# The state-space stage of an encoder trunk: the order of three engines written out in the source, in place of the scheduler's

## The chip, the cores and the metric

The kernel runs on one core of a Trainium2 chip. Its time is the device time of one execution in microseconds (us). TensorE multiplies matrices, VectorE, ScalarE and GpSimd work on tiles in the on-chip memory, and SyncE issues the transfers. In the profile they are PE, DVE, ACT, POOL and SP.

## The reference

A trunk of two layers over 512 tokens of width 1024. Layer 0 is attention of two kinds, layer 1 a bidirectional state-space mixer (Mamba-2 SSD); a squared-ReLU MLP follows each, and each residual sum is normalised. The change is in layer 1's mixer:

```
z, xbc, dt = split(x @ w_in)
xs, bm, cm = split(silu(conv5(xbc)))          # 32 heads of 64, 8 groups, state 128
dt = softplus(dt + dt_bias);  a = dt * -exp(a_log)
per direction (forward, backward), chunks of 128 tokens, acum = cumsum(a):
  y_diag = ((C B^T) * exp(acum_l - acum_s), masked) @ (xs * dt)
  states = B^T (xs * dt * exp(acum_end - acum))
  prev   = scan over chunks: prev * exp(acum_end) + states
  y_off  = exp(acum) * (C @ prev)
y = y_f + y_b + xs * d_skip;  y = rmsnorm_per_group(y * silu(z)) * norm_w;  return y @ w_out
```

## The kernel before

Everything lies transposed (features on partitions, the 512 tokens along the free axis). Each float32 operand is split into a high and a low part (`w_hi` on ScalarE, line 69; `w_lo` on VectorE or, for some listed chunks, GpSimd, line 70), and each product is three matmuls (lines 209 to 211). Weight chunks are prepared three ahead, in four buffers.

The input projection is a stream of *steps*: one step is the three matmuls of one contraction block (`project_steps`), eight steps make one 128 x 512 tile. The function `stream` issues the projections of the group after the current one and, behind each, the five-tap convolution (`conv`, line 801 on ScalarE and four instructions of line 803 on VectorE) and the SiLU. The state-space work of the eight groups is put between these steps: `wait()` runs the stream up to the next number in `times` and then issues the next piece of the group's matmuls. A group has 48 steps, the first has more.

A group's pieces in their order are: the product of B and C (line 1031, copied to `cb`); transposes of B (`btok`) and of the two x tiles (`xtok`); `xw`, x weighted by decay and step (line 1054); the states of the three chunk borders (line 1064) with their running sum `pv` (line 1072 on GpSimd, line 1075 on VectorE); four products with the states (line 1006), each multiplied by the decay rows `r` (line 1009); two products within the chunks (line 1016) of `xtok` and `m`, which is `cb` times a decay matrix `e` (line 997); the sum `y` (lines 1019 to 1022); the gate with `z` (line 1106); and the group's normalisation (`scaled`), spread over the next group: squares summed into `q` (line 925), matmuls of the sums, `rstd`, a trip through memory (`rs_d`) to get a row on all partitions, and the scaling of line 961.

A decay matrix `e` is made for each of a group's four heads by `decay_inner`: two loads of `r` from memory (line 872), a mask added on GpSimd (`tb`, line 876), eight exponentials on ScalarE (line 882), and a sum on GpSimd (line 884). `decay_rows` loads and exponentiates the rows `r` (lines 901 and 903).

TensorE's order is the order of the source (`manual_schedule` around the whole body). The order on VectorE, ScalarE, GpSimd and SyncE is chosen by the framework's scheduler when the kernel is built; only ScalarE's table functions are chained in source order by `pin`.

## Time and profile before

| | |
|---|---|
| time, median of 3 runs | 1491.42 us (1489.56 to 1492.58) |
| the profiled execution | 1490.02 us, span 1488.2 us |
| mean granted TensorE clock | 0.977 of full speed |
| TensorE busy | 1407.4 us, 95% |
| VectorE busy | 847.3 us, 57% |
| ScalarE busy | 638.3 us, 43% |
| GpSimd busy | 368.6 us, 25% |

The span runs from the first to the last instruction of the profile. The state-space stage lies between about 620 and 1070 us of it. A granted clock of 1.00 is 2.4 GHz, and a stretch with a mean below 1 ran in part at 1.2 GHz. "Busy" for TensorE takes in matmuls at the low clock, which last longer.

### The profile page before, as it was taken

The numbers are of one execution on the slowest core, as the hardware profiler recorded it, in microseconds if no ns is written. First come the engines' busy times: TensorE is split into PE (matmuls) and PEld (weight loads), VectorE is DVE, ScalarE is ACT, GpSimd is POOL, SyncE is SP. The second block draws the span as 40 slices with busy tenths as digits, with TensorE's granted clock in tenths as the row PEclk, the third lists the DMA queues.
The fourth block names the chain that finished last, engine by engine and source line by source line (L and its number), as shares of the span: only waits on it lengthen the run. The fifth ranks groups of instructions, "written<-read, shape, count | busy, mean of one in ns | idle before, by whom it ended". The sixth has DMA issues, their size and how long they took to land.

```text
span 1488.2 us, 18931 instructions
## 1 busy us (share of the span) xinstructions
PE 1407.4 (95%) x7200; PEld 1160.5 (78%) x7200; DVE 847.3 (57%) x1231; ACT 638.3 (43%) x1117; POOL 368.6 (25%) x255
## 2 busy tenths in 40 slices
PE   8899998999999999987988998999998999999998
PEld 7777778888888888866766876777888888888886
DVE  4677577344343337577678678767467344343336
ACT  5688633323132231467466556645414323142220
POOL 1354221000000121065354466353323100000000
PEclk9999999999999999999999999989999999999999
DMA  8322255223143212374443434432436333133101
GB/s 283 102 95 65 69 198 170 88 97 100 57 127 99 79 43 74 109 184 120 129 127 110 128 113 132 111 97 66 151 97 227 99 99 99 57 127 99 57 1 57
DMA packets 62403, 161.50 MB, mean 109 GB/s; under 512 B 9612, under 2 KB 19624, under 8 KB 62312
## 3 DMA queue, kind: packets, MB, share of 16 engines
q1 hardware_dynamic: 62312, 160.29, 34.4%
q8 instruction: 57, 0.93, 0.2%
q14 instruction: 34, 0.28, 0.1%
HBM read 154.87 MB, written 5.39 MB: 108 GB/s over the span
## 4 chain that ended last, share of the span: by engine, by line
PE 41%; DVE 8%; ACT 4%; issue 2%; DMA 1%; POOL 1%; SPq 0%; DVEq 0%; ACTq 0%; POOLq 0%
PE mm L209 10%; PE mm L210 9%; PE mm L211 9%; PE b L211 2%; PE b L210 2%; PE b L209 2%; DVE xw L1054 2%; PE aux L1064 2%; ACT tb L882 2%; DVE xs L803 1%; PE y L1006 1%; DVE w_lo L70 1%; PE y L1016 1%; DVE m L997 1%; DMA q<-rs_d 1%
## 5 line engine op out<-in xcount | busy, mean ns | idle before, releaser
L69 ACT ACTIVATE w_hi<-w_raw 128x1024 fp32r<-128x1024 f32 (+1 forms) x220 | 231.3, 1053 | 548.4 <-PE mm L210 244.1
L209 PE MATMUL mm<-hi,w_hi 128*128 128x512 f32 (+2 forms) x1112 | 429.8, 387 | 0.6 <-ACT hi L231 0.5
L210 PE MATMUL mm<-lo,w_hi 128*128 128x512 f32 (+2 forms) x1112 | 419.1, 377 | 10.8 <-DVE lo L232 10.8
L211 PE MATMUL mm<-hi,w_lo 128*128 128x512 f32 (+2 forms) x1112 | 417.3, 375 | 0.0
L70 DVE TENSOR_TENSOR w_lo<-w_raw,w_hi 128x1024 fp32r<-128x1024 f32 (+1 forms) x182 | 230.6, 1269 | 294.7 <-ACT w_hi L69 289.9
L210 PEld LDWEIGHTS mm<-lo,w_hi 128*128 128x128 f32 (+1 forms) x1112 | 212.3, 191 | 44.9 <-DVE lo L232 11.5
L209 PEld LDWEIGHTS mm<-hi,w_hi 128*128 128x128 f32 (+1 forms) x1112 | 212.2, 191 | 41.0 <-issue 5.5
L211 PEld LDWEIGHTS mm<-hi,w_lo 128*128 128x128 f32 (+1 forms) x1112 | 211.3, 190 | 39.5
L70 POOL TENSOR_TENSOR w_lo<-w_raw,w_hi 128x1024 fp32r<-128x1024 f32 (+1 forms) x38 | 92.3, 2434 | 445.4 <-ACT w_hi L69 442.2
L209 PE MATMUL mm<-w_hi,hi 128*128 128x512 f32 x352 | 141.1, 401 | 5.9 <-ACT hi L171 5.2
L211 PE MATMUL mm<-w_hi,lo 128*128 128x512 f32 x352 | 139.3, 396 | 0.0
L210 PE MATMUL mm<-w_lo,hi 128*128 128x512 f32 x352 | 139.2, 396 | 0.0
L210 PE MATMUL b<-w_lo,hi 128*128 128x512 f32 (+1 forms) x328 | 123.5, 377 | 1.2 <-DVE w_lo L70 1.2
L209 PE MATMUL b<-w_hi,hi 128*128 128x512 f32 (+1 forms) x328 | 123.6, 377 | 0.4 <-DVE res L310 0.4
L211 PE MATMUL b<-w_hi,lo 128*128 128x512 f32 (+1 forms) x328 | 123.5, 376 | 0.0
L336 POOL TENSOR_TENSOR rstd<-ve,half 128x1 f32<-128x1 f32 x16 | 13.7, 854 | 330.9 <-DVE neg L334 312.2
L876 POOL TENSOR_TENSOR tb<-r,dmask 128x1024 f32<-128x1024 f32 x32 | 84.0, 2626 | 25.7 <-DMA r<-ac_d 24.4
L209 PEld LDWEIGHTS mm<-w_hi,hi 128*128 128x128 f32 x352 | 66.9, 190 | 20.8 <-ACT hi L171 5.2
L211 PEld LDWEIGHTS mm<-w_hi,lo 128*128 128x128 f32 x352 | 66.7, 189 | 15.8 <-DVE lo L232 0.4
L882 ACT ACTIVATE tb<-tb,ac_tok 128x128 f32<-128x128 f32 x256 | 77.6, 390 | 0.6 <-POOL tb L876 0.5
L210 PEld LDWEIGHTS mm<-w_lo,hi 128*128 128x128 f32 x352 | 66.8, 190 | 14.1
L384 DVE TENSOR_TENSOR sq<-relu 128x512 f32<-128x512 f32 x64 | 60.3, 943 | 28.7 <-ACT relu L382 28.7
(279 smaller groups left out, 1860.5 us busy)
## 6 DMA issues: line engine op xcount, KB each, us to landing
w_raw<-in_w_m_dram SPq DMA_DIRECT2D x128, 512.0 KB, 3.6
w_raw<-in_w_ssm_dram SPq DMA_DIRECT2D x48, 512.0 KB, 3.6
r<-ac_d SPq DMA_DIRECT2D x64, 256.0 KB, 4.2
w_raw<-in_w_so_dram SPq DMA_DIRECT2D x16, 512.0 KB, 3.7
w_raw<-in_w_att_dram SPq DMA_DIRECT2D x14, 512.0 KB, 5.4
r<-ac_d SPq DMA_DIRECT2D x64, 96.0 KB, 3.1
w_raw<-in_w_ao_dram SPq DMA_DIRECT2D x8, 512.0 KB, 3.6
xraw<-in_xT_dram SPq DMA_DIRECT2D x8, 256.0 KB, 6.6
```

Source lines behind the costliest of these rows:

```text
L69: split = [nc.scalar.activation(hi[:, cols], raw[:, cols], AF.Copy), eng.tensor_tensor(lo[:, cols], raw[:, cols], hi[:, cols].bitcast(F32) ...
L70: eng.tensor_tensor(lo[:, cols], raw[:, cols], hi[:, cols].bitcast(F32), op=ALU.subtract)]
L209: PE.matmul(ps, lhs_h, rhs_h, start=first, stop=False)
L210: PE.matmul(ps, lhs_h, rhs_l, start=False, stop=False)
L211: PE.matmul(ps, lhs_l, rhs_h, start=False, stop=last)
L384: DVE.tensor_tensor(s, r, r, op=ALU.mult)
L803: DVE.scalar_tensor_tensor(acc[:, lo_o:lo_o + n], ps[:, lo_i:lo_i + n], cw[:, i, k:k + 1], acc[:, lo_o:lo_o + n], op0=ALU.mult, op1=ALU.add)
L876: POOL.tensor_tensor(x, r.rearrange("p d (c l) -> p d c l", c=NT), bc(dmask.unsqueeze(2), [P, 2, NT, P]), op=ALU.add)
L882: pin(ACT.activation(x[:, d, c, :], x[:, d, c, :], AF.Exp, bias=ac_tok[:, c, 32 * d + hf:32 * d + hf + 1]))
L997: DVE.tensor_tensor(m, cb, es[h], op=ALU.mult)
L1054: DVE.tensor_tensor(t, x_tok[j][:, d:d + 3, :].rearrange("p c (h e) -> p c h e", h=2), bc(wdec[:, d:d + 3, hd:hd + 2].unsqueeze(3), [P, 3, ...
L1064: PE.matmul(ps[:, d * 256 + j * P:d * 256 + j * P + P], b_tok[:, c, :], xw[j, d][:, c - d, :, :].rearrange("p h e -> p (h e)"), start=True ...
```

## The change

In the state-space stage VectorE, ScalarE and GpSimd now also run in source order (`manual_schedule` with four engines around `ssd`); SyncE does not. So that source order can differ from the order in which the code reads, pieces of work are queued by `later(step, fn)` and issued when the stream has reached that step (`due`). `decay_inner` and `decay_rows` become lists of pieces with steps for loading, masking, exponentiating and summing. SiLUs, gates, `xw`, `m` and the parts of the normalisation get steps of their own. The steps of TensorE's pieces move: in a group from the second on, the three chunk states go from 13, 13 and 18 to 18, 19 and 22 and the four products with the states from 27, 27, 37 and 38 to 30, 31, 39 and 40. In the output projection that follows, the first split of `y` stays ahead of the sweep and the next eight, which stood there with it, are issued one every third step. The arithmetic stays the same.

```
+        at = [0]
+        tasks = []
+        def due():
+            while tasks and tasks[0][0] <= at[0]:
+                tasks.pop(0)[2]()
+        def later(step, fn):
+            tasks.append((step, len(tasks) and max(t[1] for t in tasks) + 1, fn))
+            tasks.sort(key=lambda t: t[:2])
+        def fill_to(n):
+            while at[0] < n:
+                due()
+                next(steps, None)
+                at[0] += 1
+            due()
...
-                    z = wk.tile([P, T], F32, name="z", bufs=2)
-                    pin(ACT.activation(z, zs[j], AF.Silu))
-                    tiles["z", g, j] = z
+                    later(base + (0 if g == 0 else 33 if g < G - 1 else 2 + 6 * j), lambda g=g, j=j, ps=zs[j]: gate(g, j, ps))
                 if g == 0:
                     for j in range(2):
                         yield from convolved(j, "xs", 4, ("x", 0, j))
-                        silu(tiles["x", 0, j])
+                        later(at[0] + 6, lambda j=j: silu(("x", 0, j)))
                     yield from convolved(17, "bt", 2, ("b", 1))
                     yield from convolved(25, "ct", 2, ("c", 1))
                 if g + 1 < G:
-                    silu(tiles["b", g + 1])
-                    silu(tiles["c", g + 1])
+                    for n in "bc":
+                        later(base + (41 if g == 0 else 34), lambda n=n, g=g: silu((n, g + 1)))
                     for j in range(2):
                         yield from convolved(2 * (g + 1) + j, "xs", 4, ("x", g + 1, j))
-                        silu(tiles["x", g + 1, j])
+                        later(base + (38, 46)[j], lambda j=j, g=g: silu(("x", g + 1, j)))
...
+        def decay_inner(g, h, load, mask, exp, total):
+            hf = 4 * g + h
+            v = {}
+            def loads():
+                v["r"] = wk.tile([P, 2, T], F32, name="r", bufs=2)
                 for d in range(2):
+                    nc.sync.dma_start(out=v["r"][:, d, :],
                                       in_=ac_d[32 * d + hf:32 * d + hf + 1, :].partition_broadcast(P))
+            def masks():
+                v["x"] = wk.tile([P, 2, NT, P], F32, name="tb", bufs=2)
+                POOL.tensor_tensor(v["x"], v["r"].rearrange("p d (c l) -> p d c l", c=NT),
                                    bc(dmask.unsqueeze(2), [P, 2, NT, P]), op=ALU.add)
+            def exps(d, c):
+                pin(ACT.activation(v["x"][:, d, c, :], v["x"][:, d, c, :], AF.Exp,
+                                   bias=ac_tok[:, c, 32 * d + hf:32 * d + hf + 1]))
+            def sums():
+                es[g, h] = wk.tile([P, NT, P], F32, name="e", bufs=6)
+                POOL.tensor_tensor(es[g, h], v["x"][:, 0], v["x"][:, 1], op=ALU.add)
+            later(load, loads)
+            later(mask, masks)
+            for i in range(8):
+                later(exp + i // 2, lambda i=i: exps(i // NT, i % NT))
+            later(total, sums)
...
+        fill_to(12)
+        dt_sums()
+        later(30, dt_exps)
+        for g in range(G):
+            o = 16 + 48 * g
+            if g == 0:
+                for h, at_steps in enumerate(((14, 20, 31, 36), (15, 23, 35, 40), (25, 37, 40, 45), (26, 41, 45, 50))):
+                    decay_inner(0, h, *at_steps)
+                decay_rows(0, 0, 30, 47)
+                decay_rows(0, 1, 31, 48)
+                decay_inner(1, 0, 38, 46, 50, 56)
+                decay_inner(1, 1, 42, 51, 64, 69)
+                decay_rows(1, 0, 55, 69)
+                decay_rows(1, 1, 60, 69)
+                continue
+            if g > 1:
+                decay_rows(g, 1, o - 6, o + (20 if g == G - 1 else 1))
+            n = 4 if g in (1, G - 1) else 0
+            for h in range(2):
+                p = o + 5 * h + n
+                decay_inner(g, 2 + h, o - 7 + 4 * h, p, p + 6, p + 11)
+                if g + 1 < G:
+                    decay_inner(g + 1, h, p + 7, p + 12, p + 17, p + 22)
+            if g + 1 < G:
+                decay_rows(g + 1, 0, o + 20, o + 31)
...
-            times = iter(tuple(352 + n for n in (1, 4, 6, 7, 10, 12, 19, 21, 25, 28, 32, 32, 33, 41)) if g == G - 1 else
-                         (9, 21, 25, 37, 45, 47, 47, 49, 51, 51, 51, 54, 57, 58) if g == 0 else
-                         [16 + 48 * g + n for n in (0, 0, 4, 6, 13, 13, 18, 22, 27, 27, 31, 37, 38, 44)])
+            o = 16 + 48 * g
+            times = iter([o + n for n in (
+                (0, 5, 8, 16, 28, 29, 30, 32, 35, 36, 39, 41, 42, 44, 46, 48) if g == 0 else
+                (0, 0, 3, 5, 12, 16, 18, 19, 22, 27, 30, 31, 35, 39, 40, 45))])
...
+                def gated(g=g):
+                    DVE.tensor_tensor(y, y, tiles.pop(("z", g, j)), op=ALU.mult)
+                later(at[0] + 5, gated)
...
+                later(o + 7, lambda norm=norm: next(norm))
...
-            ms = [inner(0)]
...
+                    later(max(at[0] + 1, 31), lambda j=j, d=d: weighted(j, d))
+            for _ in range(2):
+                wait()
+                if g > 0:
+                    next(norm)
...
+            for h in range(3):
+                later(at[0] + 1 + h, lambda h=h: inner(h))
             wait()
             if g > 0:
-                norm = scaled(g - 1, ys)
                 next(norm)
-                next(norm)
-            if g + 1 < G:
-                next_es = decay_inner(g + 1, range(2))
-            if g > 0:
-                es += decay_inner(g, range(2, 4))
+                later(at[0] + 10, lambda norm=norm: run(norm))
...
-            ms.append(inner(1))
             wait()
             ys = [within(0)]
-            if g + 1 < G:
-                next_rs = decay_rows(g + 1)
+            later(at[0] + 1, lambda: inner(3))
...
-            for i in range(8):
-                split_y(y_tiles[1 + i], hs[i], ls[i])
             begun.extend([mm_bank() for _ in range(NT)])
             for n, _ in enumerate(sweep_lead(yh, yl, begun, 8, 16)):
-                if n >= 12 and n % 4 == 0 and len(yh) < min(16, len(y_tiles)):
-                    split_y(y_tiles[len(yh)], *next(spare))
+                if n % 3 == 0 and len(yh) < min(16, len(y_tiles)):
+                    i = len(yh)
+                    split_y(y_tiles[i], *((hs[i - 1], ls[i - 1]) if i < 9 else next(spare)))
...
+            E = mybir.EngineType
+            with tc.manual_schedule(engines={E.PE, E.Activation, E.DVE, E.Pool}):
+                ys = ssd(st, main, banks, first_sweep)
```

## Rows read from the trace of the kernel before

**Rows 1.** The page's first part: busy time, share and instructions by engine.

```profile
PE 1407.4 (95%) x7200; PEld 1160.5 (78%) x7200; DVE 847.3 (57%) x1231; ACT 638.3 (43%) x1117; POOL 368.6 (25%) x255
```

**Rows 2.** Windows cut at each group's product of B and C.

```profile
core 0: us, PE busy (x) PEld busy (x) DVE busy (x) ACT busy (x) POOL busy (x), PEclk, DMA share, GB/s
628.20:690.80 62.60, 50.85 (x256) 41.81 (x257) 45.17 (x53) 37.05 (x79) 36.04 (x18) 0.92 0.55 145
690.80:743.50 52.70, 46.70 (x256) 38.37 (x255) 37.21 (x45) 32.96 (x63) 25.23 (x16) 0.94 0.44 134
...
1006.30:1062.00 55.70, 52.66 (x298) 42.75 (x298) 33.89 (x46) 26.17 (x49) 21.90 (x15) 1.00 0.23 72
```

**Rows 3.** Windows of the fifth group, cut behind its third chunk state.

```profile
848.90:873.20 24.30, 20.59 (x99) 17.39 (x98) 23.93 (x25) 18.77 (x44) 17.27 (x12) 0.86 0.41 125
873.20:899.80 26.60, 26.60 (x159) 21.43 (x158) 13.92 (x21) 12.88 (x19) 8.69 (x6) 1.00 0.40 119
```

**Rows 4.** Waits of TensorE in the stage, 628 to 1062 us.

```profile
engine line waited for: us in total, times, longest us
PE aux L1064 <- DVE xw L1054: 34.0, 13, 5.3
PE y L1006 <- DVE pv L1075: 7.0, 2, 5.7
```

**Rows 5.** Timeline of TensorE at the chunk states: start, us, instruction, [idle before].

```profile
863.79 1.22 PE L1064 MATMUL aux<-xw,btok 128*128 128x128 f32 x4 [3.39 <-DVE xw L1054]
...
872.42 1.05 PE L1064 MATMUL aux<-xw,btok 128*128 128x128 f32 x8
873.23 0.48 PE L209 MATMUL mm<-hi,w_hi 128*128 128x512 f32 x1
```

**Rows 6.** Windows of ten microseconds, the one with these states.

```profile
860.00:870.00 10.00, 6.29 (x23) 5.31 (x22) 9.93 (x8) 5.53 (x18) 7.95 (x5) 0.69 0.41 125
```

**Rows 7.** Timeline of VectorE ahead of the states.

```profile
851.50 1.22 DVE L70 TENSOR_TENSOR w_lo<-w_raw,w_hi 128x1024 fp32r<-128x1024 f32 x1
...
855.97 0.91 DVE L925 TENSOR_TENSOR q<-q,q 128x512 f32<-128x512 f32 x1
...
858.24 7.03 DVE L1054 TENSOR_TENSOR xw<-xtok,wdec 128x384 f32<-128x384 f32 x4
```

**Rows 8.** Single lines, 736 to 1000 us: durations in ns, least/median/most.

```profile
L1054 DVE TENSOR_TENSOR xw<-xtok,wdec x20: 544/1464/2699, 756.5 to 970.2; 128x384 f32<-128x384 f32 x20
...
L997 DVE TENSOR_TENSOR m<-cb,e x20: 681/692/2901, 750.5 to 991.3; 128x512 f32<-128x512 f32 x20
...
L925 DVE TENSOR_TENSOR q<-q,q x5: 911/1583/2769, 754.4 to 963.0; 128x512 f32<-128x512 f32 x5
```

**Rows 9.** Timeline of GpSimd while the `xw` ran.

```profile
860.78 2.54 POOL L876 TENSOR_TENSOR tb<-r,dmask 128x1024 f32<-128x1024 f32 x1
```

**Rows 10.** Windows, a stretch of the second MLP.

```profile
1200.00:1300.00 100.00, 100.00 (x435) 81.39 (x435) 37.35 (x41) 26.47 (x33) 2.41 (x1) 1.00 0.27 84
```

**Rows 11.** Lines by form, VectorE, 736 to 1000 us: busy us, mean ns, idle before.

```profile
L803 DVE SCALAR_TENSOR_TENSOR bt<-mm,cw,bt 128x511 f32<-128x511 f32 x10 | 7.5, 745 | 0.1
...
L1106 DVE TENSOR_TENSOR hi<-hi,z 128x512 f32<-128x512 f32 x5 | 3.4, 687 | 0.2 <-POOL hi L1022 0.2
L913 DVE COPY btok<-aux 128x512 f32<-128x512 f32 x5 | 3.4, 681 | 0.0
```

**Rows 12.** Lines by form, GpSimd, 736 to 1000 us.

```profile
L876 POOL TENSOR_TENSOR tb<-r,dmask 128x1024 f32<-128x1024 f32 x20 | 51.0, 2551 | 0.8
L884 POOL TENSOR_TENSOR e<-tb 128x512 f32<-128x512 f32 x20 | 32.1, 1607 | 20.7 <-ACT tb L882 16.1 <-DMA r<-ac_d 4.7
...
L1072 POOL TENSOR_TENSOR pv<-pv,cdec 128x512 f32<-128x512 f32 x10 | 12.3, 1233 | 14.8 <-ACT pv L1070 14.2 <-DVE pv L1075 0.5
...
L944 POOL TENSOR_TENSOR rstd<-rstd,half 128x4 f32<-128x4 f32 x5 | 5.1, 1019 | 20.6 <-DVE rstd L943 20.6
```

**Rows 13.** Lines by form, ScalarE, 736 to 1000 us.

```profile
L882 ACT ACTIVATE tb<-tb,ac_tok 128x128 f32<-128x128 f32 x160 | 48.5, 390 | 0.1
...
L813 ACT ACT_TABLE_LOAD x5 | 6.4, 1283 | 0.1
```

**Rows 14.** The loads `r` of line 872, 736 to 1000 us.

```profile
DMA to landing us min/median/max: 3.0/4.3/5.5
```

More of the change, by code (lines that the diff above doesn't have):

```diff
@@ L835, in spare, with gate @@
             yield [late.tile([P, T], F32R, name="m", bufs=3) for _ in range(2)]
+        def gate(g, j, ps):
+            z = wk.tile([P, T], F32, name="z", bufs=2)
+            pin(ACT.activation(z, ps, AF.Silu))
+            tiles["z", g, j] = z
         def stream():
             for g in range(G):
+                base = 16 + 48 * g
                 if 0 < g < G - 1:
@@ L890, in decay_inner @@
-                es.append(e)
-            return es
-        def decay_rows(g):
-            rs = []
-            for j in range(2):
-                r2 = late.tile([P, 2, 384], F32, name="r2", bufs=3)
+            def exps(d, c):
[4 more added lines that the diff above has]
+                POOL.tensor_tensor(es[g, h], v["x"][:, 0], v["x"][:, 1], op=ALU.add)
@@ L897, in decay_rows, with loads @@
+            later(load, loads)
[3 more added lines that the diff above has]
+            later(total, sums)
+        def decay_rows(g, j, load, exp):
+            r2 = []
+            def loads():
+                r2.append(late.tile([P, 2, 384], F32, name="r2", bufs=3))
                 for d in range(2):
@@ L900, in decay_rows, with exps @@
                         c0 = P - P * d
-                        nc.sync.dma_start(out=r2[64 * q:64 * q + 64, d, :],
+                        nc.sync.dma_start(out=r2[0][64 * q:64 * q + 64, d, :],
                                           in_=ac_d[row:row + 1, c0:c0 + 384].partition_broadcast(64))
-                pin(ACT.activation(r2, r2, AF.Exp))
-                rs.append(r2)
-            return rs
+            def exps():
+                pin(ACT.activation(r2[0], r2[0], AF.Exp))
+                rs[g, j] = r2[0]
+            later(load, loads)
+            later(exp, exps)
         def to_tok(src, name, dve=False):
@@ L953, in scaled @@
                 nc.sync.dma_start(out=row, in_=rs_d[g:g + 1, :].partition_broadcast(P))
+                yield
             else:
@@ L965, in ssd @@
         steps = stream()
-        first_exps = []
-        at = [0]
-        def fill(n):
-            for _ in range(n):
-                next(steps, None)
-            at[0] += n
-        def fill_to(n):
-            fill(max(0, n - at[0]))
         for i, (col, name) in enumerate(((16, "bt"), (24, "ct"))):
             tiles[name[0], 0] = conv(banks[1 + i], col, name, 2)
-        dt_sums(fill)
         for name in "bc":
-            silu(tiles[name, 0])
-        es = decay_inner(0, range(2))
+            later(3, lambda name=name: silu((name, 0)))
@@ L990, in wait, with inner @@
             def wait():
                 fill_to(next(times))
[L993 to L999 removed]
+            def inner(h):
+                m = late.tile([P, NT, P], F32, name="m", bufs=3)
+                DVE.tensor_tensor(m, cb, es.pop((g, h)), op=ALU.mult)
+                ms.append(m)
@@ L1001, in from_states, with weighted @@
+            def weighted(j, d):
+                t = late.tile([P, 3, 2, 64], F32, name=f"xw{j}{d}", bufs=1)
+                hd = 32 * d + 4 * g + 2 * j
+                DVE.tensor_tensor(t, x_tok[j][:, d:d + 3, :].rearrange("p c (h e) -> p c h e", h=2),
+                                  bc(wdec[:, d:d + 3, hd:hd + 2].unsqueeze(3), [P, 3, 2, 64]), op=ALU.mult)
+                xw[j, d] = t
             def from_states(j, d):
@@ L1089, in ssd @@
             from_states(0, 1)
-            if g > 0:
-                next(norm)
-            ms.append(inner(1))
             wait()
             ys = [within(0)]
-            if g + 1 < G:
-                next_rs = decay_rows(g + 1)
+            later(at[0] + 1, lambda: inner(3))
             wait()
-            if g > 0:
-                run(norm)
             from_states(1, 0)
@@ L1104, in ssd @@
             ys.append(within(1))
-            for j in range(2):
-                DVE.tensor_tensor(ys[j], ys[j], tiles.pop(("z", g, j)), op=ALU.mult)
-            if g + 1 < G:
-                es, rs = next_es, next_rs
         norm = scaled(G - 1, ys)
+        fill_to(at[0] + 7)
         next(norm)
-        fill(12)
+        fill_to(at[0] + 6)
         next(norm)
-        fill(4)
+        fill_to(at[0] + 5)
         run(norm)
+        fill_to(at[0] + 80)
         run(steps)
```

63 lines of the change are left out of this document (15 added, 48 removed).

## The prediction, made before the changed kernel was run

> **What bounds the kernel now.** The page's shares come first: TensorE is busy for 1407.4 of 1488.2 us, VectorE for 57% and ScalarE for 43% [rows 1]. TensorE's own work is the same before and after, so only two things can shrink the time: its idle stretches, and stretches in which it counts as busy at a low granted clock. Windows cut at each group's first product of B and C (the matmuls of line 1031) show where these lie [rows 2]. The first state-space group takes 62.6 us with 50.85 us busy, the next 52.7, both at a mean clock of 0.92 to 0.94; the eighth is at 1.00 and idle for 3.0 us (55.70 less 52.66). From the second group's start to the eighth's lie 1006.3 - 690.8 = 315.5 us for six groups, 52.6 each.
>
> Cutting one group in two tells more [rows 3]. From its start to behind the third chunk state it has 18 projection steps in 24.3 us, busy 20.59, clock 0.86. The remaining 30 steps take 26.6 us, busy all the time at clock 1.00. So the loss lies ahead of and around the chunk states (line 1064), and the waits name the cause: matmuls of line 1064 waited 34.0 us in 13 waits for the weighted inputs `xw` of line 1054, and the products with the states 7.0 us for `pv`; every other entry is smaller [rows 4]. In the group cut above TensorE stands for 3.39 us ahead of one of these matmuls [rows 5]; the ten us around it have clock 0.69, so a good part of them ran at 1.2 GHz instead of 2.4 [rows 6].
>
> VectorE is not idle while this happens: four `xw` take 7.03 us, behind a `q` [rows 7]. `xw` takes between 0.544 and 2.699 us, `m` between 0.681 and 2.901, `q` between 0.911 and 2.769, the same shapes each time [rows 8], and while the four `xw` ran GpSimd was at work too, 2.54 us on one mask alone [rows 9]. So VectorE's work ahead of the states is both ordered late and stretched.
>
> **What the clean time would be.** In a stage with nothing but projection matmuls 435 of them take 100 us, 0.23 us each [rows 10], so a step of three is 0.69 us. The clean second half of the group is measured, 26.6 us. The first half has 18 steps, 12.4 us, and 45 of its 99 matmuls are small ones [rows 3]. Eight of them take 0.81 us, from their start at 872.42 to that of the next projection matmul at 873.23 [rows 5], so 0.10 each: 4.5 us. First half clean: about 17.0. A group: 43.6. Six groups: 262, against 315.5, so 54 us can be had there. The first group has 55 steps from its product on, 7 more (4.8 us) and no normalisation of a group before it (some 1 us): 47.5 clean against 62.6, so 15. The eighth: its 3.0 idle. Altogether 72 us, of which no schedule can give more unless it also empties stalls outside this stage.
>
> **The change part by part.** No arithmetic is added or removed; the sums below are about what stands ahead of what.
>
> *Chunk states later.* Their three steps go from 13, 13, 18 to 18, 19, 22 of a group. The first comes 5 steps, 3.4 us, later, about the 3.39 us of the wait above. Later is not free: the first product with the states goes only from step 27 to 30, so the chain of states to products shrinks from 9 steps to 8.
>
> *VectorE's order.* Ahead of the states now stand only what they need and what TensorE needs. I walk a group from its product of B and C (time 0). The product and transpose end at about 1.3. In source order VectorE then does: `cb` 0.68, `btok` 0.68, four convolution instructions of 0.74, one `w_lo` of 1.22, the gate 0.69, four `xw` at their unstretched 0.544, `q` 0.911 [rows 7, 8, 11]: 9.3 us, from about 1.0 to 10.3. The two `m` that stood here go behind the states (three at steps 23 to 25, the fourth at 36). TensorE reaches the norm's sums (step 12), which need `q`, at 12 x 0.69 + 1.3 + 0.7 = 10.3: level. It reaches the first state (step 18) at about 14.8, when the last `xw` is 5 us old. So the big wait goes, and what is late next is `q`, by nothing to a few us.
>
> *From the states to the products.* VectorE has the next convolution (3.0), two `w_lo` (2.4) and `rstd` until about 15.5, then waits for the states. Here GpSimd's order counts. Its queue is mask, mask, then (exponentials of the first head done at about 11) sum, mask, sum, `rstd`, mask, `pv`, sum, `pv`, sum; with 2.55 for a mask, 1.61 for a sum, 1.23 for a `pv` and 1.02 for `rstd` [rows 12] from 11.2 on that puts the second `pv` at about 11.2 + 1.61 + 2.55 + 1.61 + 1.02 + 2.55 + 1.23 + 1.61 + 1.23 = 24.6, VectorE's addition at 25.3, and TensorE's first product with the states (step 30) at about 26. A margin of under 1 us; VectorE stands in its queue meanwhile, with three `m` and a `w_lo` behind it. Those (3 x 0.68 + 1.22) end at 28.6 and the multiplications of the products' results follow; TensorE needs the bank for the product within the chunks at about 30.5. Met, by 1 to 2 us. In the rest of the group VectorE has two convolutions, two `w_lo`, two `y`, `m`, two scalings, four `r` and a gate, about 15.5 us for the 15 us that are left, so it goes into the next group some 1 to 2 us late.
>
> *ScalarE.* The 32 exponentials (0.39 us each [rows 13]) and all the rest come to 31.6 us in the group cut above [rows 3], of 43.6. The exponentials now stand together ahead of step 32 and the SiLUs behind it, so two table loads of 1.28 us [rows 13] go from four a group. I cost this at nothing: ScalarE idles some 20 us of a group now. If that cover were gone, it would be 2.6 us a group in the change's favour.
>
> *GpSimd and SyncE.* GpSimd's masks are issued seven steps or so behind their loads `r`. A load lands in 3.0 to 5.5 us [rows 14]; seven steps with the products in them are 6 or 7. Each head issues its two DMAs, each pair of rows four more, as before; the first mask is needed by step 6 only, another 4 us. The row of scales is loaded from step 27 and used at 37, 10 us. SyncE is not fixed by the source, and its queue carries the same DMAs. I cost them at nothing; a load late by more than some 5 us would show as `q` or `xw` late.
>
> *First group.* Loads and exponentials are spread from step 14 to 53. From step 31 to 48 ScalarE has about 18 us of work while TensorE has 14, and the chain `pv`, addition, `pv`, addition behind it has no slack: I take 5 us of TensorE wait, between 1 and 10.
>
> *Last group.* The eight splits ahead of the output projection become one every third step. The first split now stands directly ahead of the matmuls that read it (a copy and a subtraction, 0.6 and 0.7 us, behind the queue), so I take the 3 us of idle time there as staying.
>
> **The sum.** From 72 I take off 5 for the first group, 6 for the six groups (1.0 each: `q` level at step 12, VectorE 1 to 2 us late at the border), 3 for the last: 58. The profiled execution took 1490.02 us (its span of 1488.2 and 1.8 around it), 1.4 below the median of the runs, 1491.42. So 1432 against the profiled execution, **1433 us** against the median, about 3.9% less.
>
> **Rivals.**
>
> *The stretch stays.* What speaks for it: the same GpSimd instructions run, 26 us of each 51 in the cut-out group [rows 3], and VectorE can no longer step round one. By the rows an `xw` behind a mask gains up to 2.2 us, and two masks back to back would cost 5.1 us ahead of `q`, which has no margin. With half of that in each group (2.5), and again the low clock behind it as now (about as much loss as the wait itself), the six groups keep 5 each, 30 instead of 6: 1457 us, 1445 to 1475. Against it: in the walk GpSimd has done its two masks by 5.1 and idles until 11, just where the `xw` lie. The Trainium skill ("SBUF — State Buffer", section "Who interferes with whom") has a rule for this: a VectorE instruction with two SBUF inputs and a GpSimd instruction that reads SBUF share one read port, and whichever starts second waits for the whole of the other. This trace agrees: `xw` at most 2.699, which is its 0.544 and little less than one mask. By that rule a fixed order can meet a mask with each `xw`, and the case above is what it would give here.
>
> *The wait moves whole.* TensorE stops at the norm's sums or at the first product with the states for as long as at line 1064 now: about 1490, no change. Both have margins of less than 1 us. Against: what VectorE loses ahead of the states, two `m` and the stretch, falls into a part that is clean and half empty (VectorE 13.92 of 26.60 [rows 3]).
>
> *Slower.* The place is the second addition into `pv`: VectorE waits there for GpSimd, which stands behind masks that wait for tiles that ScalarE must first release. The margin is about 1 us; every us beyond it stops VectorE, and by the products' banks TensorE. To be slower than before it must give back all 58 us, 9.7 a group, that is, the second `pv` must come 10.7 us late. That is more than four masks' length, and nothing in the rows stretches GpSimd so far. At 12 us late the time is 1433 + 6 x 11 = 1499.
>
> **How the numbers follow.** Forecast 0.66 (1418 to 1447 by the bounds of the first group, 1 to 10, the last, 0 to 4, and 0 to 2.5 a group); stretch stays 0.21; moved whole 0.06; slower 0.07. The range of 8 in 10 takes the forecast and most of the second case: 1417 to 1467. A difference of 0.2%, 3 us, is about what a measurement of this kernel can tell from none. Faster by more than that: 0.66 + 0.21 and a little of the third, 0.88; same 0.05; slower 0.07.
>
> **What would show it.** Right: the a group's period, from one product of B and C to the next, of 44 to 45 us with clock 0.98 or more; waits of the states' matmuls for `xw` gone; `xw` near 0.55 and two table loads a group. Wrong: TensorE waiting for `q` at the norm's sums or for `pv` at the products, and slices of 0.7 clock once in each group; then the second case holds, or the third if the period stays at 52. Slower needs GpSimd's `pv` far behind its step.

## The result and the profile after

The changed kernel takes **1453.36 us** (median of 4 runs, 1450.29 to 1454.23) against 1491.29 for the kernel before on the same chip: a ratio of 0.9743, interval 0.9724 to 0.9761. The direction and the range held. The time is 20 us above the forecast of 1433 and above the 1418 to 1447 that the likeliest case alone had given; it lies within the 1445 to 1475 of the rival "the stretch stays", for which the range had been widened. 38 us were saved, not 58.

The first part of the page after, to be held against [rows 1]:

```profile
PE 1394.9 (96%) x7200; PEld 1151.6 (79%) x7200; DVE 848.9 (58%) x1231; ACT 620.4 (43%) x1105; POOL 369.6 (25%) x255
```

The same TensorE instructions are busy 12.5 us less, as less of them runs at the low clock (mean 0.987, before 0.977). ScalarE has 12 instructions fewer, the table loads below. VectorE's busy time has not fallen: what it saved in one place it lost in another (below).

Windows of the kernel after, cut as in [rows 2] at each group's product of B and C (now line 1093):

```profile
630.90:685.30 54.40, 46.82 (x246) 38.25 (x244) 40.12 (x48) 37.20 (x74) 28.14 (x15) 0.94 0.60 170
685.30:733.10 47.80, 45.47 (x257) 37.27 (x256) 39.53 (x46) 28.79 (x64) 26.62 (x16) 0.96 0.43 125
733.10:780.30 47.20, 45.48 (x255) 37.40 (x254) 39.88 (x47) 29.22 (x60) 25.20 (x15) 0.96 0.46 134
780.30:826.40 46.10, 44.09 (x256) 36.16 (x255) 36.13 (x46) 28.80 (x59) 28.96 (x17) 1.00 0.44 137
...
917.00:962.10 45.10, 43.87 (x255) 36.20 (x254) 38.69 (x43) 28.32 (x59) 32.77 (x18) 1.00 0.48 152
962.10:1020.00 57.90, 52.28 (x279) 41.87 (x278) 42.03 (x47) 27.20 (x51) 25.86 (x16) 0.94 0.22 62
```

A group from the second to the seventh takes 45 to 48 us where it took 51 to 54, and four of the six run at clock 1.00 throughout. Between the same marks as in the prediction, the two profiled spans (1488.2 and 1452.4, 35.8 apart) compare as follows. The first product stands four steps (2.8 us) later in the stream than before: between it and the next, each of the lines 209 to 211 now runs 48 times, before 52 times. So the first two stretches are taken together; the eighth's product stands one step (0.7 us) earlier, which is left as it is.

| stretch | saving predicted | measured |
|---|---|---|
| up to the second group's product | 10 (15 less 5) | 690.8 - 685.3 = 5.5 |
| six groups | 48 (54 less 6) | 315.53 - 276.85 = 38.7 |
| from the eighth group's product to the end | 0 (3 less 3) | 481.9 - 490.3 = -8.4 |
| sum | 58 | 35.8 |

So all three residuals were set too small. The waits of TensorE in the stage name them:

```profile
PE aux L962 <- DVE q L957: 9.2, 6, 2.3
PE mm L211 <- DVE ct L232: 5.4, 1, 5.4
PE y L1059 <- DVE pv L1131: 5.1, 1, 5.1
PE aux L1120 <- DVE xw L1050: 1.4, 2, 0.8
```

The 34.0 us that the chunk states waited for `xw` [rows 4] have become 1.4. In their place stand one wait for `q` in each of the six groups, and one long stop each in the last group (for the first split of `y`, line 232) and in the first (for `pv`).

**One group.** The sixth, cut behind its chunk states as [rows 3] cut the fifth of before:

```profile
871.40:893.70 22.30, 20.66 (x119) 17.21 (x118) 17.94 (x20) 16.60 (x37) 20.15 (x10) 1.00 0.58 166
893.70:917.00 23.30, 23.30 (x139) 19.05 (x138) 19.62 (x25) 12.35 (x22) 7.36 (x7) 1.00 0.36 114
```

The whole of its idle time, 1.64 us, is the wait for `q`. TensorE's, VectorE's and GpSimd's timelines there:

```profile
883.67 0.43 PE L962 MATMUL aux<-q,ones 128*32 128x128 f32 x8 [1.64 <-DVE q L957]
```

```profile
876.71 2.22 DVE L1080 TENSOR_TENSOR lo<-lo,z 128x512 f32<-128x512 f32 x1
878.85 4.16 DVE L1050 TENSOR_TENSOR xw<-xtok,wdec 128x384 f32<-128x384 f32 x4
882.93 0.68 DVE L957 TENSOR_TENSOR q<-q,q 128x512 f32<-128x512 f32 x1
```

```profile
876.00 2.38 POOL L70 TENSOR_TENSOR w_lo<-w_raw,w_hi 128x1024 fp32r<-128x1024 f32 x1
878.34 2.85 POOL L903 TENSOR_TENSOR tb<-r,dmask 128x1024 f32<-128x1024 f32 x1
```

VectorE is never idle on the way from `cb` to `q`. The gate takes 2.22 us instead of 0.69 beside GpSimd's `w_lo`, the four `xw` 4.16 instead of 2.18 because one of them runs beside a mask. Over five groups, `xw` and `q` as single lines (least, median, most in ns):

```profile
L1050 DVE TENSOR_TENSOR xw<-xtok,wdec x20: 543/546/2753, 742.8 to 927.6; 128x384 f32<-128x384 f32 x20
...
L957 DVE TENSOR_TENSOR q<-q,q x5: 679/679/680, 744.7 to 928.1; 128x512 f32<-128x512 f32 x5
```

and lines by form, VectorE, then ScalarE's table loads:

```profile
L70 DVE TENSOR_TENSOR w_lo<-w_raw,w_hi 128x1024 fp32r<-128x1024 f32 x24 | 43.3, 1805 | 0.0
...
L1080 DVE TENSOR_TENSOR lo<-lo,z 128x512 f32<-128x512 f32 x5 | 9.1, 1816 | 0.0
L994 DVE SCALAR_TENSOR_TENSOR hi<-hi,nw,q 128x512 f32<-128x512 f32 x6 | 8.7, 1494 | 0.0
L1080 DVE TENSOR_TENSOR hi<-hi,z 128x512 f32<-128x512 f32 x5 | 7.8, 1563 | 0.0
```

```profile
L933 ACT ACT_TABLE_LOAD x5 | 6.4, 1283 | 0.1
L856 ACT ACT_TABLE_LOAD x5 | 6.4, 1283 | 0.1
```

The median `xw` fell from 1464 to 546 ns [rows 8] and `q` is not stretched in these five groups. But the stretch has not gone, it has moved: to the gates (means 1816 and 1563 ns; those of `hi` took 687 before [rows 11], those of `lo` 1122), to `w_lo` (mean 1805; before, 24 of them took 1358) and to the scalings of line 994 (1494; before 749), which now run beside GpSimd's additions into `y`, where before nothing of GpSimd's stood. GpSimd runs the same 20 masks in five groups, and what stands beside them on VectorE is now another instruction: of the ten gates, five had nothing of GpSimd's beside them and took 0.67 to 0.68 us, the other five ran beside a mask or a `w_lo` and took 2.2 to 2.9.

**The last group.** VectorE's timeline, GpSimd's, TensorE's, then the ten us around them as a window:

```profile
966.05 2.87 DVE L1080 TENSOR_TENSOR lo<-lo,z 128x512 f32<-128x512 f32 x1 [1.02 <-POOL lo L1077]
968.84 6.29 DVE L1050 TENSOR_TENSOR xw<-xtok,wdec 128x384 f32<-128x384 f32 x4
975.06 0.68 DVE L957 TENSOR_TENSOR q<-q,q 128x512 f32<-128x512 f32 x1
975.66 0.68 DVE L232 TENSOR_TENSOR ct<-hi,bt 128x512 fp32r<-128x512 f32 x1
```

```profile
965.97 2.40 POOL L70 TENSOR_TENSOR w_lo<-w_raw,w_hi 128x1024 fp32r<-128x1024 f32 x1
968.33 5.45 POOL L903 TENSOR_TENSOR tb<-r,dmask 128x1024 f32<-128x1024 f32 x2
```

```profile
976.39 0.80 PE L211 MATMUL mm<-w_hi,ct 128*128 128x512 f32 x1 [5.44 <-DVE ct L232]
```

```profile
970.00:980.00 10.00, 4.38 (x12) 3.15 (x12) 8.68 (x9) 6.26 (x13) 3.78 (x2) 0.73 0.25 81
```

The split that the output projection needs (line 232, 0.68 us) stands behind a gate, four `xw` and `q`, 9.8 us of work beside two masks and a `w_lo` of GpSimd. TensorE stops for 5.44 us and runs part of what follows at 1.2 GHz.

**The first group.** GpSimd's queue is packed from 652 us on; its end, and TensorE's first product with the states:

```profile
660.92 3.25 POOL L903 TENSOR_TENSOR tb<-r,dmask 128x1024 f32<-128x1024 f32 x1
664.13 1.04 POOL L1128 TENSOR_TENSOR pv<-pv,cdec 128x512 f32<-128x512 f32 x1
...
666.49 2.35 POOL L903 TENSOR_TENSOR tb<-r,dmask 128x1024 f32<-128x1024 f32 x1
668.80 1.04 POOL L1128 TENSOR_TENSOR pv<-pv,cdec 128x512 f32<-128x512 f32 x1
```

```profile
671.57 0.80 PE L1059 MATMUL y<-ct,pv 128*128 128x128 f32 x2 [5.14 <-DVE pv L1131]
```

### The profile page after: what moved, and what is told of

Read it like the earlier page. It is cut to its first block, busy times and chain, and to the rows that moved or that the text cites. A ratio compares the mean times of both kernels' runs of the same rounds, so it can differ in the third digit from the quotient of the medians.

```text
span 1452.4 us, 18906 instructions
## 1 busy us (share of the span) xinstructions
PE 1394.9 (96%) x7200; PEld 1151.6 (79%) x7200; DVE 848.9 (58%) x1231; ACT 620.4 (43%) x1105; POOL 369.6 (25%) x255
## 4 chain that ended last, share of the span: by engine, by line
PE 77%; DVE 10%; issue 5%; POOL 4%; DMA 3%; ACT 1%; SPq 1%; DVEq 0%; POOLq 0%; ACTq 0%
PE mm L209 18%; PE mm L210 18%; PE mm L211 18%; PE b L211 4%; PE b L210 4%; PE b L209 4%; POOL tb L903 2%; DVE res L343 1%; DVE xw L1050 1%; DVE xs L802 1%; PE y L1059 1%; DVE w_lo L70 1%; DMA r<-ac_d 1%; PE aux L1120 1%; DVE bt L802 1%
## 5 line engine op out<-in xcount | busy, mean ns | idle before, releaser
L70 DVE TENSOR_TENSOR w_lo<-w_raw,w_hi 128x1024 fp32r<-128x1024 f32 (+1 forms) x182 | 244.1, 1343 | 261.9 <-ACT w_hi L69 261.3
L336 POOL TENSOR_TENSOR rstd<-ve,half 128x1 f32<-128x1 f32 x16 | 12.5, 783 | 332.0 <-DVE neg L334 312.9
L907 ACT ACTIVATE tb<-tb,ac_tok 128x128 f32<-128x128 f32 x256 | 81.1, 390 | 21.5 <-POOL tb L903 21.5
```

What stands on the lines that cost most here:

```text
L70: eng.tensor_tensor(lo[:, cols], raw[:, cols], hi[:, cols].bitcast(F32), op=ALU.subtract)]
L907: pin(ACT.activation(v["x"][:, d, c, :], v["x"][:, d, c, :], AF.Exp, bias=ac_tok[:, c, 32 * d + hf:32 * d + hf + 1]))
```

## The experiments

Two theories stood against each other at the start. *Order*: the gain comes from VectorE, ScalarE and GpSimd running in source order, and what is still lost is set by what stands ahead of `q`, `pv` and the split in their queues. *Later*: the gain comes from the chunk states standing five steps later in TensorE's stream. Each kernel has its median, its ratio to the kernel before on the same chip, and the stretches of its profiled execution, cut at the same products:

| kernel | us | ratio, interval | to first product | first group | six groups | from the eighth on |
|---|---|---|---|---|---|---|
| before | 1491.29 | 1 | 628.2 | 62.6 | 315.5 | 481.9 |
| after | 1453.36 | 0.9743 (0.9724 to 0.9761) | 630.9 | 54.4 | 276.9 | 490.3 |
| e1 | 1488.24 | 0.9986 (0.9972 to 1.0000) | 625.1 | 65.4 | 313.0 | 482.0 |
| e2 | 1448.28 | 0.9716 (0.9697 to 0.9736) | 626.6 | 54.3 | 276.5 | 486.7 |
| e3 | 1486.62 | 0.9972 (0.9959 to 0.9984) | 632.4 | 55.3 | 311.1 | 490.1 |
| e4 | 1454.78 | 0.9772 (0.9738 to 0.9806) | 627.9 | 53.7 | 283.9 | 487.6 |
| e5 | 1449.24 | 0.9724 (0.9709 to 0.9739) | 629.4 | 53.7 | 277.3 | 487.7 |
| e6 | 1447.90 | 0.9718 (0.9704 to 0.9733) | 625.9 | 52.7 | 275.7 | 490.1 |
| e7 | 1456.44 | 0.9773 (0.9756 to 0.9790) | 625.7 | 54.3 | 283.9 | 486.8 |
| e8 | 1460.87 | 0.9809 (0.9790 to 0.9828) | 629.7 | 53.8 | 288.5 | 486.8 |
| e9 | 1442.73 | 0.9686 (0.9669 to 0.9702) | 626.4 | 49.2 | 281.3 | 484.1 |
| e10 | 1443.51 | 0.9696 (0.9678 to 0.9714) | 626.6 | 52.7 | 276.6 | 485.7 |
| e11 | 1460.59 | 0.9807 (0.9790 to 0.9824) | 628.9 | 52.7 | 292.5 | 483.8 |
| e12 | 1452.16 | 0.9759 (0.9744 to 0.9775) | 627.8 | 52.7 | 279.2 | 489.4 |

One thing has to be read off this table before the rest. Up to the first product e2 and e4 to e12 issue the same work as the kernel after, and it ends between 625.7 and 630.9 us. So some 5 us of any difference between two profiled spans can lie ahead of everything that was edited, and an edit is judged by its own stretch. The medians were not taken side by side either: the kernel before took 1488.2 to 1491.3 us beside them, so two changed kernels are better compared by their ratios. By these e2, e5 and e6 lie 4.0, 2.8 and 3.7 us below the kernel after, with intervals that overlap its own; of the faster ones only e9 and e10 (7.0 us) lie clear of it.

### e1: the kernel before, with the states later and nothing else

```
-            times = iter(... [16 + 48 * g + n for n in (0, 0, 4, 6, 13, 13, 18, 22, 27, ...)])
+            times = iter(... [16 + 48 * g + n for n in (0, 0, 4, 6, 18, 19, 22, 22, 27, ...)])
```

> The kernel before with one edit: in the second to seventh groups the chunk states go from steps 13, 13, 18 to 18, 19, 22; the scheduler still orders the three engines. Theory 'order' (the gain comes from what VectorE has ahead of the states): the scheduler sees a later need and puts other work ahead of xw, so most of the wait at the states stays; 1470 to 1490 us, waits of the states for xw above 15 us. Rival 'later' (the five steps, 3.4 us, cover the wait by themselves): the 34 us of wait and the low clock behind it go; 1440 to 1455 us, waits of the states below 5 us.

1488.24 us, at most 0.28% under the kernel before. The waits of TensorE:

```profile
PE aux L1064 <- DVE xw L1054: 26.6, 14, 3.7
...
PE aux L930 <- DVE pv L1075: 4.3, 2, 3.5
```

The wait for `xw` shrank by a fifth, and in two groups TensorE stopped at the norm's sums instead. Later alone is worth next to nothing. In the scheduler's order VectorE still reaches `xw` late, and stretched: the median of 20 is 1630 ns.

### e2: the kernel after, with the states early

```
-                (0, 0, 3, 5, 12, 16, 18, 19, 22, 27, 30, ...))])
+                (0, 0, 3, 5, 12, 13, 13, 16, 18, 27, 30, ...))])
```

(The norm's transpose then goes between the second and the third state.)

> The changed kernel with the chunk states of the second to eighth groups back at steps 13, 13, 18 (the norm's transpose goes behind the second state, step 16). Theory 'order': the xw are ready when the norm's sums are, so the states barely wait; 1448 to 1460 us, waits of the states for xw below 6 us. Rival 'later': the wait at the states returns, some 2.5 us a group and the low clock; 1475 us or more.

1448.28 us; the six groups take 276.5 us against 276.9. Its waits of TensorE:

```profile
PE aux L962 <- DVE q L957: 7.8, 6, 2.4
...
PE aux L1123 <- DVE xw L1050: 1.4, 2, 0.8
```

With the states back at step 13 TensorE waits for `xw` no longer than in the kernel after: the order brings it in time for step 13 too. The later states contribute nothing here. The 5 us between the two medians are no gain of early states either: in the profiled executions (8.4 apart) they lie ahead of the first product (4.3) and in the last group (3.6), where the stop for the split was 2.8 us long instead of 5.4.

### e3: the kernel after, with only TensorE's order fixed

```
-            with tc.manual_schedule(engines={E.PE, E.Activation, E.DVE, E.Pool}):
+            with tc.manual_schedule(engines={E.PE}):
```

> The changed kernel with only TensorE in source order: all steps as changed, but the scheduler orders VectorE, ScalarE and GpSimd again (the chain of table functions stays). Theory 'order': 1470 to 1495 us. Rival 'later': the steps carry the gain, 1445 to 1460 us.

1486.62 us; the six groups take 311.1. Waits, then `xw` as a single line:

```profile
PE aux L962 <- DVE q L957: 19.2, 6, 6.7
PE y L1059 <- DVE pv L1131: 6.7, 4, 2.3
PE aux L1120 <- DVE rstd L975: 5.4, 5, 1.5
```

```profile
L1050 DVE TENSOR_TENSOR xw<-xtok,wdec x20: 545/1634/2752, 755.3 to 968.0; 128x384 f32<-128x384 f32 x20
```

With every step of the new source in place and VectorE, ScalarE and GpSimd left to the scheduler, all but 3 to 4 of the 38 us are gone and the median `xw` is stretched again. e1 to e3 together settle the first question: the fixed order of the three engines is the cause, the later states are not. No run fixes one of the three alone, so which engine's order does how much of it is not shown.

### e4: the norm's sums later

```
-                (0, 0, 3, 5, 12, 16, 18, 19, 22, 27, 30, ...))])
+                (0, 0, 3, 5, 15, 17, 18, 19, 22, 27, 30, ...))])
```

> The changed kernel with the norm's sums and transpose at steps 15 and 17 in place of 12 and 16. Theory 'q level': TensorE's 9.2 us of wait for q in six groups goes and nothing takes its place, since the states at 18 had no wait; 1440 to 1446 us, clock of the groups up to 1.00. Rival 'the wait moves on' (VectorE's lateness, not the place of the sums, sets the period): 1450 to 1456 us, with new waits at the states or for pv.

1454.78 us, six groups 283.9, that is 7 longer. The wait for `q` is gone, others have come:

```profile
PE aux L1120 <- DVE rstd L975: 10.9, 5, 2.4
...
PE aux L968 <- ACT q L965: 4.2, 5, 1.8
```

The sums' bank (a part of the memory that TensorE writes) is reused by the states, and it comes free only when VectorE has made `rstd` from it. VectorE has the next convolution and `w_lo` ahead of that. The reading that `q` alone was late by 1.5 us, and that a later step would give this back, fell.

### e5: the first split of `y` early

```
+                if g == G - 1:
+                    sweep = finish(y_tiles, spare())
+                    later(base, lambda: next(sweep))
...
-            yield from finish(y_tiles, spare())
+            yield from sweep
```

(A `yield` stands behind the first split.)

> The changed kernel with the first split of y issued at the start of the last group in place of directly ahead of the matmuls that read it. Theory 'split in the queue' (the last group's 5.4 us stop and the low clock behind it come from VectorE's queue ahead of that split): the stop goes; 1444 to 1450 us. Rival (VectorE is late there anyway and TensorE stops at the norm's sums or the states as long): 1452 to 1455 us.

1449.24 us, 4.1 below the kernel after in the medians. The stop of 5.4 us is gone, and TensorE now waits 1.9 us for `q` in the last group. From the eighth product on it takes 487.7 us, 2.6 less. But e2, e4, e7 and e8 keep the split where it was and take 486.7 to 487.6: there VectorE came into the last group earlier and the stop was only 2.8 to 3.2 us. So the queue ahead of the split is shown as the cause of the stop; what the edit saves is not told from that scatter.

### e6: the second group's masks later

```
-                decay_inner(1, 0, 38, 46, 50, 56)
-                decay_inner(1, 1, 42, 51, 64, 69)
+                decay_inner(1, 0, 38, 52, 56, 61)
+                decay_inner(1, 1, 42, 53, 64, 69)
```

> The changed kernel with the two masks that the first group makes for the second at steps 52 and 53 in place of 46 and 51, behind both pv multiplications in GpSimd's queue (exponentials and sums of the first of them follow, 56 and 61). Theory 'GpSimd's queue ahead of pv': the first group's 5.1 us wait for pv shrinks to under 2 us; 1445 to 1450 us. Rival (ScalarE's and VectorE's queues are as late, or the masks are then late for the second group): 1452 to 1457 us.

1447.90 us. The wait for `pv` in the first group fell from 5.1 to 3.4 us, and that group from 54.4 to 52.7. That is the 1.7 us that the edit has for itself; of the 8.0 between the two profiled executions, 5.0 lie ahead of the first product. Masks ahead of `pv` in GpSimd's queue are a part of that wait, not the whole.

### e7: `q` early

```
-                later(at[0] + 5, gated)
+                if j == 1 and g < G - 1:
+                    gates.append(gated)
+                else:
+                    later(at[0] + 5, gated)
...
-                later(o + 7, lambda norm=norm: next(norm))
+                later(o + 4, lambda norm=norm: next(norm))
...
+            for gated in gates:
+                gated()
```

(This stands directly behind `btok`.)

> The changed kernel with the second gate of a group moved ahead of the next convolution on VectorE (directly behind btok) and the norm's squares and q from step 7 to step 4, ahead of the xw. Theory 'q stands too far back': the 9.2 us of wait for q at the norm's sums go, with no wait at the states (xw later by one q); 1440 to 1447 us. Rival 'VectorE is late as a whole': the wait goes to the states or stays; 1451 to 1456 us.

1456.44 us, six groups 283.9. The wait for `q` is down to 1.2 us in all, and the next one in line has grown:

```profile
PE aux L1127 <- DVE rstd L975: 14.3, 6, 2.9
```

### e8: one of the masks moved behind the `xw`

```
-                decay_inner(g, 2 + h, o - 7 + 4 * h, p, p + 6, p + 11)
+                if 1 < g < G - 1 and h == 1:
+                    decay_inner(g, 3, o - 3, o + 11, o + 12, o + 16)
+                else:
+                    decay_inner(g, 2 + h, o - 7 + 4 * h, p, p + 6, p + 11)
```

> The changed kernel with the mask of a group's fourth head (third to seventh groups) behind GpSimd's first sum of the group (step 11 in place of 5; exponentials from 12, sum at 16), so that no mask lies beside VectorE's gate and xw. Theory 'stretch': q comes 2 us earlier in those groups and its wait goes there; 1440 to 1448 us, provided the addition into pv, up to 2.5 us later, still meets the products. Rival: the mask moved on meets w_lo and delays pv as much; 1452 to 1458 us.

1460.87 us, above the ranges of both theories; six groups 288.5. All `xw` of the groups concerned now take 0.546 to 0.555 us, and `q` is waited for once, 2.3 us. But ScalarE's timeline shows the new stop:

```profile
890.38 0.69 ACT L907 ACTIVATE tb<-tb,ac_tok 128x128 f32<-128x128 f32 x2 [3.79 <-POOL tb L903]
890.99 0.26 ACT L965 ACTIVATE q<-aux 128x128 f32<-128x128 f32 x1
```

The exponentials wait for the moved mask, and behind them in the fixed order stands the copy of the norm's sums (line 965), for which TensorE's next transpose waited 12.4 us in five groups.

### e9: GpSimd without the masks' reads

```
-                POOL.tensor_tensor(v["x"], v["r"].rearrange("p d (c l) -> p d c l", c=NT),
-                                   bc(dmask.unsqueeze(2), [P, 2, NT, P]), op=ALU.add)
+                POOL.memset(v["x"], -3000.0)
```

> The changed kernel with GpSimd's masks replaced by a fill with a constant into the same tile (the mask and the cumulative sums of the row are left out of the decay matrices), so GpSimd reads nothing there and is done sooner; the order on TensorE, VectorE and ScalarE is unchanged. Theory 'stretch' (what makes VectorE late for q is that gate, xw and w_lo wait for masks): the 9.2 us of wait for q go, and the first group's wait for pv shrinks; 1430 to 1442 us. Rival 'VectorE's own count of work': q still waits 6 us or more over the six groups, only the first group gains; 1445 to 1452 us.

1442.73 us. Windows of the third and the seventh group, and VectorE's lines by form:

```profile
737.60:781.45 43.85, 43.85 (x255) 36.21 (x254) 35.05 (x47) 28.92 (x59) 18.13 (x15) 1.00 0.31 97
...
913.00:956.90 43.90, 43.90 (x256) 36.22 (x256) 33.76 (x45) 28.95 (x60) 26.30 (x20) 1.00 0.36 108
```

```profile
L70 DVE TENSOR_TENSOR w_lo<-w_raw,w_hi 128x1024 fp32r<-128x1024 f32 x24 | 30.3, 1261 | 2.7 <-ACT w_hi L69 2.7
...
L1080 DVE TENSOR_TENSOR lo<-lo,z 128x512 f32<-128x512 f32 x5 | 3.4, 677 | 0.0
```

Five groups have no idle time of TensorE at all, with the same order in the source on TensorE, VectorE, ScalarE and GpSimd. That is the clean group: 43.85 us, 43.6 in the prediction. The gate is at 677 ns, `w_lo` at 1261. The edit has a cost of its own: loads `r` that no mask reads any more run ahead in SyncE's queue (the DMA engines are busy for 0.77 of the second group, 0.31 to 0.36 of the next five), ScalarE waits 17.9 us for another one in that second group (62.0 us), and TensorE waits 15.8 us for `q` there. So by estimate the time understates the gain by 62.0 - 43.9 = 18 us. The edit also shortens GpSimd's work (a fill takes 0.955 us, a mask 2.56). So it shows that the masks cost the groups their residual; by itself it does not tell the stretch from their length.

### e10 to e12: combinations

e10 is e2, e5 and e6 in one; e11 is e10 with e8's mask; e12 is e5, e6 and the moved mask with its exponentials one step later:

```
+                    decay_inner(g, 3, o - 3, o + 11, o + 13, o + 16)
```

> The changed kernel with three of the edits together: chunk states at 13, 13, 18; first split of y at the start of the last group; the first group's two masks behind pv. By themselves they took off 5.1, 4.1 and 5.5 us. If they lie in different places (second to seventh, last and first group) they add: 1437 to 1441 us. If they share a cause: 1443 to 1449 us.

> The three edits together and the fourth head's mask behind GpSimd's first sum (step 11). Theory 'stretch': another 5 us or more off the three, 1430 to 1436 us. Rival (pv and w_lo then as late as q was): no better than the three together.

> The changed kernel (states at 18, 19, 22) with the first split of y early, the first group's two masks behind pv, and the fourth head's mask behind GpSimd's first sum as in the kernel of the moved mask, but its exponentials from step 13 in place of 12, so that they stand behind the copy of the norm's sums in ScalarE's queue. Theory 'order in the queue' (the moved mask cost time only because ScalarE stood at its exponentials with that copy behind them): neither q nor the copy is waited for, 1432 to 1440 us. Rival (GpSimd's chain, 2 to 3 us later, makes pv late for the products instead): 1444 to 1452 us, with waits of the products with the states for pv in five groups.

e10 takes 1443.51 us, 0.9696 of the kernel before, the best of the kernels that leave nothing out; that is 9.9 us below the kernel after in the medians and 7.0 by the ratios. The six groups are as they were (276.6); of the rest, 1.7 us are the first group's, 4.6 the last one's, and 4.3 lie ahead of the first product. The time fell into the range set for a shared cause, but the stretches show none: e5 and e6 act in different places, and the gains of e2 and e6 that were to be added held 4 to 5 us each, in their profiled executions, from ahead of the first product. e11 gives all of it back in the six groups (292.5); TensorE waits 17.2 us there for the copy of the norm's sums. In e12 the copy no longer stands behind the exponentials, and the six groups (279.2) come back to within 2.3 us of the kernel after, but the wait has moved once more, to `pv`:

```profile
PE aux L984 <- DVE pv L1137: 7.4, 5, 2.3
```

Line 984 there is the transpose of `rstd` at step 27, which takes a bank that the states had used, and that bank is free only after VectorE's addition into `pv`. The products with the states, which the expectation had named, did not wait in these groups.

## Why the prediction came out as it did

**The cause.** Right: the fixed order removes the wait for `xw` (34.0 to 1.4 us), and `q` is late next. That VectorE's part of it does this, as the prediction has it, is argued and not run alone. Two things changed ahead of the states: the two `m` (0.7 us each) left VectorE's queue there, and GpSimd's masks and sums no longer run beside the `xw`, but for one. Of 20 `xw` in five groups, 14 had a GpSimd instruction beside them before and took up to 2.70 us; after the change one has (2.75 us), and the other 19 take 0.54 to 0.55. So the argument against the rival, that GpSimd idles where the `xw` lie, held for the `xw`.

**"Chunk states later".** This step failed. The prediction set the 3.4 us of five later steps against the 3.39 us of the wait, as if they were a part of the gain. Alone it left the wait at 26.6 us (e1), and without it none returned (e2).

**The clean group.** Right: 43.6 predicted, 43.85 in five groups of e9. So TensorE's own work leaves the six groups 52 to 54 us to gain; no kernel here that keeps the masks came nearer than 39.8 (e6).

**The residual of the six groups.** Predicted 6 us, measured 276.9 - 6 x 43.6 = 15. Of these 10.0 are idle time, nearly all of it the wait for `q` (9.2 in six waits), and 3.1 the two groups at clock 0.96 (45.5 busy, 43.9 in the clean ones); the rest is the difference between 43.6 and the 43.9 to 44.1 that the other four are busy. The mis-sized term is "`q` level": the walk gave every instruction ahead of `q` its unstretched price. In the group shown, the gate and the `xw` take 1.5 and 2.0 us more than that, yet VectorE ended `q` only 12.2 us after the product, not 10.3: of the 3.5 us, 1.2 are covered by a `w_lo` that the walk gave to VectorE and that GpSimd does in this group, and 0.2 by `q` (0.911, measured 0.68). In the third, fourth, fifth and seventh groups VectorE does that `w_lo` itself, and there it and the gate are lengthened by 2.0 to 2.5 us together. The walk had put GpSimd's two masks at the group's start, done by 5.1, and had it idle until 11. In fact two additions into `y` come first, and in the third to seventh groups the second mask ends 7.5 to 9.8 us after the product; in the group shown it ran from 878.34 to 881.19, beside the `xw`. The rival "the stretch stays" had this mechanism at 5 us a group; it came at 2.5, since the idle time was 1.7 us a group and four groups kept the clock.

**From the states to the products.** Right, and closely: the second addition into `pv` was to end at 25.3 us of a group; in the sixth it ended at 897.07 + 0.69 - 871.40 = 26.4, and no product waited for it. The margin that the prediction called thin was there; where GpSimd's queue was made later (e12), the first wait for `pv` came not at the products but three steps earlier, at the transpose of `rstd`, which the prediction had not looked at.

**Table loads and GpSimd's loads.** Table loads went from four a group to two as predicted; ScalarE's busy time fell by 17.9 us, and no wait tells of it. GpSimd stood idle for 0.4 us in all ahead of its 20 masks in five groups, so the loads `r` came in time.

**The first group.** Two things are off here. The prediction counted 55 steps from the product on, 7 more than a group; the trace of the kernel before has 52 there, 4 more. By the prediction's own prices its clean time is then 43.6 + 2.8 - 1 = 45.4 us and not 47.5, and 17 us could be had, not 15. And of these 17 it gave back 11.7 (17.2 less 5.5), where 5 had been taken, between 1 and 10. The place was right, `pv`, 5.1 us of waiting, 7.6 us of idle time in all; what was not costed is the low clock behind the stop (the window's mean is 0.94), by estimate the other 4 us. Nothing of this lies ahead of the first product in these two executions: it comes 2.6 us later, for four steps of 0.7.

**The last group.** Predicted to keep its 3 us, it lost 8.4 on top. This is the step with the largest error for its size: the split was costed at its own 0.6 and 0.7 us "behind the queue", and the queue was not counted. In it stood 9.8 us of VectorE's work, stretched too. Further on, two splits of the output projection (lines 231 and 232), which before caused no wait, stop TensorE for another 2.3 us.

**The range.** It held, but not for the reason that it was drawn for. The second case was let into it for a stretch that costs the six groups 24 us more than the forecast; there it cost 9. Of the 22 us by which the profiled saving fell short, the other 13 came from the first and the last group, where the prediction had said nothing of a stretch. That these sums stayed inside one range is in part luck.

**What stays open.** How much of the gain belongs to which engine's order. How much of a mask's harm to `pv` is stretch and how much its length (e9 takes away both). For `q` the trace of the kernel after tells it: in the third to seventh groups VectorE never idles for more than 0.04 us at a time between `cb` and `q`, so what it loses there is the lengthening of its own instructions. Why the stretch ahead of the first product differs between executions by up to 5 us. And a position for the fourth mask that serves `q`, the copy of the sums and `pv` at once was not found.

## What to carry to other kernels

Where an engine runs in the order of the source, ask of each piece of work what stands ahead of it in its queue, at the price that these have beside the other engines and not at their best one: e4, e7, e8 and e12 each removed or shrank a wait, and each time another took its place, for `rstd` (e4, e7), for the copy of the sums (e8) and for `pv` (e12). Where a change has two parts, have each tried alone before its share is believed; one of these two was worth nothing that the runs can tell. And when two kernels differ by a few us, compare the stretch that was edited, since stretches that no edit touched differed by as much.

## What the runs showed of the hardware

The same `xw` of 128x384 takes 0.546 or 2.75 us in the kernel after, depending on whether GpSimd's mask, with two inputs in the on-chip memory, runs beside it. A fill by GpSimd of the same tile, which reads nothing, does not lengthen VectorE's work: in e9 five `w_lo` and one gate began behind a fill's start and ran beside it, and they took 1.21 to 1.22 and 0.68 us, as long as those with nothing beside them, while in the kernel after a `w_lo` beside a mask took up to 3.2 us and a gate up to 2.9. And a stop does not always cost the clock: with 1.0 to 2.0 us of idle time in each, four groups stayed at 1.00, and two with 1.7 and 2.3 came to 0.96, while the stops of 5.1 and 5.4 us lie in or just ahead of stretches of 0.66 (670 to 680 us) and 0.73 (970 to 980).
